# An S5 recurrence over chunks taken in two levels, with its local part on diagonal pair blocks

## The chip, the cores and the metric

The kernel runs on one core of a Trainium2 chip as a single launch. The metric is the device time of one execution in microseconds (us); the median of several executions is compared. TensorE (PE), VectorE (DVE), ScalarE (ACT) and GpSimd (POOL) each work through their own list of instructions in order, SyncE (SP) issues most of the loads, and the engines wait for each other by semaphores.

## The reference, cut to what matters

The kernel is a two-layer decoder trunk on 256 tokens and 2048 channels: an S5 state-space layer, shared keys and values, then a sparse-attention layer. Every sub-layer is modulated by products of `c` with large weights (adaLN). The change is in the S5 layer, whose mixer is:

```python
def s5_mixer(h, ...):
    u, z = jnp.split(h @ w_in, 2, axis=-1)
    ug = u.reshape(B_, L, SSM_GROUPS, SSM_GROUP)          # 128 groups of 16 channels
    bu = einsum('blgc,gnc->blgn', ug, bb)                  # 64 complex states a group
    x = scan(x[t] = a * x[t-1] + bu[t])                    # over 256 tokens
    y = Re(einsum('blgn,gcn->blgc', x, c)) + d_skip * ug
    y = gelu(y)
    y = y * sigmoid(y @ w_glu + b_glu)
    return (y * silu(z)) @ w_out
# adaLN: shift, scale, gate = split(silu(c) @ mod_w + mod_b)
```

## The kernel before, in words

A float32 product is made of three matmuls per block of 128x128 weights and 256 tokens: the weights are split into a high part (`hi`, ACT, line 202) and a low part (`lo`, DVE, line 203), and `project_half` (lines 227 to 229) runs `hi` on the high and low parts of the activations and `lo` on the high part. A half block is 8 such triples, 24 matmuls, and needs one 512 KB load into a ring of 8 buffers (`raw`), 2 `hi` and 2 `lo`.

The adaLN products are made in blocks of 128 columns. Blocks 0 to 31 are made while u is computed. Of the rest, `PE_MODS` go to TensorE in pairs (`pe_mod_pair`, line 157, "m" in the plan; four loads of 512 KB and then two small sums at line 162), and `DVE_MODS` to VectorE (`dve_mod`, line 144, "d" in the plan; two loads and two instructions of 128x1024 a block, which need the table `cact`).

The first half of u (8 blocks) is computed row by row (`u_rows`, lines 290 to 293). While that runs, the tables of the S5 layer are made. Then comes the S5 stage proper. The 256 tokens are cut into 64 chunks of 4 tokens, and the channels into two halves, f = 0 and 1:

- `u_turn` (line 516) brings u with the channels of pairs of groups on the partitions, and `scan_in` (line 573) makes what each chunk adds to the states; ACT copies it into `VV[f]` (names `Vva`, `Vvb`).
- `scan_run` (lines 608 to 611) is the recurrence over chunks: 62 steps of four DVE instructions of 128x64, each step reading what the step before wrote.
- `scan_local` (line 623) adds what a token gets from its own chunk. Its tables are Toeplitz matrices of 64x64; they are laid out by writing `ktd` to DRAM (8 writes, line 487) and reading it back shifted (16 reads, line 587), on POOL's queue.
- `scan_out` (line 641) adds what the states carry, and `y_turn` (line 663) turns y round to channels and through the GELU. `y_split` (lines 219 and 220) makes its high and low parts for the next product, the GLU.

What fills the time of the recurrences is a plan, `PLAN`: a string for each of the slots that the program passes with `fill()`: "u" and "z" are half blocks of the projections u and z, "m" a TensorE pair, "d" a VectorE block. The plan sets the order in which instructions are handed to a scheduler; the scheduler and the tile pools set the order on each engine. In the kernel before, the second half of u is computed before the first recurrence ends, and the 16 blocks of z are spread over both recurrences; z has a tile of its own in the place of the input x (tag `zz`).

After the S5 stage come the GLU product (line 708 reads its sums), w_out (line 722; it adds to `x`, which line 718 loads again), keys and values, queries, attention, and the output.

Of the kernel before, what the change touches and what calls it, by code (L numbers as in the profile page):

```python
# [70 lines left out]
def trunk_kernel(ctx, tc, xT, crow, ccol, vec, m0n, mn, mt, w_ur, w_in, w_glu, w_out, w_kv, w_qr, w_q, w_g,  # L71
# [113 lines left out]
    # ---------------------------------------------------------------- projections  # L185
# [8 lines left out]
    def split_w(r, n):  # L194
        """The first n of the eight blocks in r, four by four."""
# [11 lines left out]
    class Act:  # L207
        """A matrix [2048 channels, 256 tokens] as a high and a low part."""
# [37 lines left out]
    def rms_scale(tot):  # L246
        """1 / sqrt(mean square over channels), for every token, on all partitions."""
# [16 lines left out]
    # ---------------------------------------------------------------- layer 0: modulation and u  # L264
# [858 lines left out]
```

## Time and profile before

| | |
|---|---|
| median of 3 runs | 1364.55 us (1359.84, 1364.55, 1367.36) |
| span of the profiled execution | 1368.1 us, clock of TensorE 0.965 of full speed on average |
| time of the profiled execution itself | not on record apart from its span |
| busy: PE, DVE, ACT, POOL | 1267.0, 1068.3, 681.7, 42.5 us |
| chain that ended last, by engine | PE 68%, DVE 15%, DMA 12%, issue 3%, ACT 2% |
| HBM traffic | 326.10 MB read, 4.72 MB written |

PE is busy for 93% of the span, but the busy time of pipelined matmuls overlaps; the table by stage in the rows below shows where it is not busy. From the trace the stages are: u row by row and tables until 157 us, the S5 stage from there to about 428 us, the GLU to 527, w_out to 618, keys and values to about 845, then queries and attention. A duration in a row is that of one instruction; since matmuls are pipelined, the cost of many is read from the distance between their starts.

### The profile page before, as it was taken

What the parts mean: (1) busy time and instruction counts of PE and PEld (TensorE: products, weight loads), DVE (VectorE), ACT (ScalarE), POOL (GpSimd) and SP (SyncE); (2) the same over time, 40 slices, a digit from 0 to 9 for tenths busy, and PEclk for the clock granted to TensorE, in tenths of its full rate; (3) what the DMA queues carried; (4) which work ended last, traced back from release to release, by engine and by line L of the source; (5) the groups of instructions that cost most, each with busy time, mean ns of one, the idle gap of its engine ahead of it and who ended that gap; (6) DMA issues with size and microseconds to landing.
All of it is one profiled execution on the core that took longest, in us unless ns stands there. A gap on an engine that the chain in (4) does not pass through costs nothing.

```text
span 1368.1 us, 31424 instructions
## 1 busy us (share of the span) xinstructions
PE 1267.0 (93%) x12270; PEld 1200.6 (88%) x12270; DVE 1068.3 (78%) x2612; ACT 681.7 (50%) x1439; POOL 42.5 (3%) x71
## 2 busy tenths in 40 slices
PE   2799979989999999997998999999999999999995
PEld 2678779878888999986997999999999999999995
DVE  5998318999997898889877878776878777777665
ACT  3345544423356555544453545555555555555653
POOL 1000500001001000000000000000000000000001
PEclk9999989999999999997899999999999999999998
DMA  9799966649788999985887888876555444444541
GB/s 359 275 347 336 316 200 200 205 172 336 242 300 299 321 357 318 327 305 187 293 303 248 277 295 289 274 253 227 170 193 194 165 144 141 159 142 161 186 155 62
DMA packets 94055, 332.88 MB, mean 243 GB/s; under 512 B 12785, under 2 KB 13025, under 8 KB 92881
## 3 DMA queue, kind: packets, MB, share of 16 engines
q1 hardware_dynamic: 91792, 321.45, 68.3%
q0 software_dynamic: 2112, 9.42, 2.1%
q8 instruction: 96, 1.57, 0.5%
q14 instruction: 55, 0.44, 0.1%
HBM read 326.10 MB, written 4.72 MB: 242 GB/s over the span
## 4 chain that ended last, share of the span: by engine, by line
PE 68%; DVE 15%; DMA 12%; issue 3%; ACT 2%; SPq 0%; DVEq 0%; ACTq 0%
PE acc L229 18%; PE acc L227 18%; PE acc L228 18%; DMA raw<-in_mt_dram 6%; DVE lo L203 3%; DMA raw<-in_w_in_dram 3%; DVE raw L144 2%; PE macc L157 2%; PE s L957 1%; DVE stab L608 1%; DMA mraw<-in_m0n_dram 1%; PE op L1008 1%; DVE stab L610 1%; PE kp L467 1%; DVE stab L609 1%
## 5 line engine op out<-in xcount | busy, mean ns | idle before, releaser
L202 ACT ACTIVATE hi<-raw 128x512 fp32r<-128x512 f32 x640 | 400.9, 631 | 466.1 <-PE acc L228 395.9
L203 DVE TENSOR_TENSOR lo<-raw,hi 128x512 fp32r<-128x512 f32 x640 | 435.0, 690 | 146.8 <-ACT hi L202 143.6
L228 PE MATMUL acc<-hq,hi 128*128 128x256 f32 x960 | 274.9, 286 | 0.0
L229 PE MATMUL acc<-hq,lo 128*128 128x256 f32 x960 | 271.5, 284 | 2.5 <-DVE lo L203 2.3
L227 PE MATMUL acc<-hq,hi 128*128 128x256 f32 x960 | 273.2, 285 | 0.4 <-ACT hi L202 0.4
L144 DVE SCALAR_TENSOR_TENSOR raw<-raw,cact 128x1024 f32<-128x1024 f32 x156 | 190.1, 1220 | 57.0 <-DMA raw<-in_mt_dram 56.6
L229 PEld LDWEIGHTS acc<-hq,lo 128*128 128x128 f32 x960 | 180.5, 189 | 5.4 <-DVE lo L203 3.9
L228 PEld LDWEIGHTS acc<-hq,hi 128*128 128x128 f32 x960 | 180.9, 188 | 3.7 <-issue 3.3
L227 PEld LDWEIGHTS acc<-hq,hi 128*128 128x128 f32 x960 | 180.9, 188 | 1.3 <-issue 0.7
L229 PE MATMUL acc<-h,lo 128*128 128x256 f32 x384 | 114.0, 297 | 12.7 <-DVE lo L203 12.3
L229 PE MATMUL acc<-hkv,lo 128*128 128x256 f32 x384 | 114.2, 299 | 5.1 <-DVE lo L203 4.6
L227 PE MATMUL acc<-hkv,hi 128*128 128x256 f32 x384 | 112.5, 295 | 4.9 <-ACT hkv L260 4.9
L227 PE MATMUL acc<-h,hi 128*128 128x256 f32 x384 | 113.5, 296 | 1.0 <-ACT hi L202 1.0
L228 PE MATMUL acc<-hkv,hi 128*128 128x256 f32 x384 | 111.9, 294 | 0.8 <-DVE hkv L261 0.8
L228 PE MATMUL acc<-h,hi 128*128 128x256 f32 x384 | 111.6, 291 | 0.0
L229 PEld LDWEIGHTS acc<-h,lo 128*128 128x128 f32 x384 | 76.1, 198 | 17.4 <-DVE lo L203 14.0
L229 PEld LDWEIGHTS acc<-hkv,lo 128*128 128x128 f32 x384 | 77.3, 202 | 7.6 <-DVE lo L203 7.2
L227 PEld LDWEIGHTS acc<-hkv,hi 128*128 128x128 f32 x384 | 77.3, 202 | 5.8 <-ACT hkv L260 5.8
L227 PEld LDWEIGHTS acc<-h,hi 128*128 128x128 f32 x384 | 76.1, 198 | 5.3 <-issue 2.5
L228 PEld LDWEIGHTS acc<-hkv,hi 128*128 128x128 f32 x384 | 77.4, 202 | 1.4 <-DVE hkv L261 1.4
L157 PE MATMUL macc<-mraw,cz 128*32 128x128 f32 x1600 | 59.0, 300 | 18.9 <-DMA mraw<-in_m0n_dram 17.9
L228 PEld LDWEIGHTS acc<-h,hi 128*128 128x128 f32 x384 | 76.1, 198 | 0.1
(312 smaller groups left out, 2829.6 us busy)
## 6 DMA issues: line engine op xcount, KB each, us to landing
raw<-in_mt_dram SPq DMA_DIRECT2D x156, 512.0 KB, 5.6
raw<-in_w_z_dram SPq DMA_DIRECT2D x96, 512.0 KB, 3.7
mraw<-in_m0n_dram SPq DMA_DIRECT2D x64, 512.0 KB, 7.8
raw<-in_w_in_dram SPq DMA_DIRECT2D x48, 512.0 KB, 6.1
raw<-in_w_kv_dram SPq DMA_DIRECT2D x48, 512.0 KB, 5.2
mraw<-in_mn_dram SPq DMA_DIRECT2D x36, 512.0 KB, 6.6
raw<-in_w_glu_dram SPq DMA_DIRECT2D x32, 512.0 KB, 6.3
raw<-in_w_out_dram SPq DMA_DIRECT2D x32, 512.0 KB, 6.1
```

Of the source, the lines that this page charges most:

```text
L144: nc.vector.scalar_tensor_tensor(out=rf, in0=rf, scalar=1.0, in1=cact[:, 1024 * e:1024 * e + 1024], op0=OP.mult, op1=OP.mult, accum_out=mo ...
L157: nc.tensor.matmul(acc[32 * j:32 * j + 32, 128 * e:128 * e + 128], cz[:, q, :], r[:, q % 8, :], start=(e == 0 and q < 4), stop=(q >= 12), ...
L202: nc.scalar.activation(hi[:, 0:c, :], rr, AF.Copy)
L203: nc.vector.tensor_sub(lo[:, 0:c, :], rr, hi[:, 0:c, :].bitcast(F32))
L227: nc.tensor.matmul(acc, hi[:, kk, :], act(0, k), start=(k == 0), stop=False)
L228: nc.tensor.matmul(acc, hi[:, kk, :], act(1, k), start=False, stop=False)
L229: nc.tensor.matmul(acc, lo[:, kk, :], act(0, k), start=False, stop=(k == KT - 1))
L467: nc.tensor.matmul(kp[32 * q:32 * q + 32, l, :], bb[r][pr, 32 * h:32 * h + 32], kc_[pr, 2 * h:2 * h + 2, r, :], start=(l == 0 and r == 0), ...
L608: V.tensor_mul(ra, VH[:, :, :, :, k], ar)
L609: V.tensor_mul(rb, VH[:, :, ::-1, :, k], ai)
L610: V.tensor_add(ra, ra, VH[:, :, :, :, k + 1])
L957: nc.tensor.matmul(sp, qo(a, h)[:, qs], kk[:, kv, b, o:o + w], start=(i == 0), stop=(i == 2))
```

## The change

The chunks are kept, but the recurrence over 64 chunks goes in two levels. The chunk index is written as i (8 values, consecutive chunks) and s (8 segments), with s innermost. `scan_run` now does seven steps along i for all eight segments at once (four DVE instructions of 128x512 each), then six small steps that carry from segment to segment (128x64), and then adds to every chunk the carry times a power of the transition (16 instructions of 128x896). The powers are made by some 48 small DVE instructions (`powers`) earlier. So that s is innermost, the tokens are held in that order from the norm on (`order`, `into`), and the result goes back to token order where w_out's sums are added to `x`.

The Toeplitz tables, `scan_local` and the traffic through DRAM go. In their place `y_turn` adds the local part by products with 32x32 diagonal blocks (`kd`), four tiles beside each other, into the same PSUM tile that holds the turned y.

u is now held in the tile of the input (`x0`), and z is written over it; z can be computed only for blocks whose `y_turn` is done. All of z comes after the recurrences: 8 blocks in one slot after `y_turn(0)`, 8 after `y_turn(1)`. The rest of u and the pairs fill the recurrences. 14 more blocks of adaLN go to TensorE (`NA` 0 to 16, `NB` 2 to 0: `PE_MODS` from 18 to 32 blocks, `DVE_MODS` from 78 to 64), and `cact` is loaded only after `y_turn(1)`. `dvec` is loaded by four small DMAs in place of one. The `x` for w_out has the tag `cb`, which before held `cbS` and now holds `scr`, the recurrence's scratch.

```diff
-NA, NB = 0, 2
+NA, NB = 16, 0
 PLAN = [
-    "zzm", "", "um", "u", "d", "z", "z", "d", "m", "z", "zu", "zz", "dm", "m", "zm", "zmz", "z", "mz", "zzzz",
...
+    "uu", "uu", "muu", "uu", "muu", "uu", "muu", "uu", "m", "", "m", "",
+    "m", "", "m", "", "", "m", "", "m", "", "m", "", "zzzzmzzzzmzzzzmzzzz", "", "", "", "m", "", "m", "", "mm",
...
+    ucm = x0.rearrange("p m (i j s) -> p m i j s", i=8, j=4)
+    scr = pool.tile([128, 4096], F32, tag="cb", name="scr")
...
     def scan_run(f):
-        for k in range(1, 63):
-            V.tensor_mul(ra, VH[:, :, :, :, k], ar)
-            V.tensor_mul(rb, VH[:, :, ::-1, :, k], ai)
-            V.tensor_add(ra, ra, VH[:, :, :, :, k + 1])
-            V.tensor_add(VH[:, :, :, :, k + 1], ra, rb)
+        def step(dst, add, src, n, t, w, u):
+            sh = (128, 2, 32, w)
+            V.tensor_tensor(ra[:, :, :, 0:w], src, QW[0][:, n, gsl].unsqueeze(1).unsqueeze(3).to_broadcast(sh), op=OP.mult)
+            V.tensor_tensor(rb[:, :, :, 0:w], u, SG[t][:, :, gsl].unsqueeze(3).to_broadcast(sh), op=OP.mult)
+            V.tensor_add(ra[:, :, :, 0:w], ra[:, :, :, 0:w], add)
+            V.tensor_add(dst, ra[:, :, :, 0:w], rb[:, :, :, 0:w])
+        for i in range(2, 9):
+            x = X[:, :, :, i % 8, :]
+            step(x, x, X[:, :, :, i - 1, :], 0, 0, 8, X[:, ::-1, :, i - 1, :])
...
+        for j in range(1, 7):
+            step(cy[:, :, :, j + 1:j + 2], X[:, :, :, 0, j:j + 1], cy[:, :, :, j:j + 1], 7, 1, 1, cy[:, ::-1, :, j:j + 1])
+        nc.scalar.activation(X[:, :, :, 0, :], cy, AF.Copy)
+        for hh in range(2):
...
+            for r in range(2):
+                x = X[:, r, g, 1:8, :]
+                for e in range(2):
+                    V.tensor_tensor(mt_, cy[:, r ^ e, g, :].unsqueeze(2).to_broadcast(sh), pw[e], op=OP.mult)
+                    V.tensor_tensor(x, x, mt_, op=OP.subtract if e and not r else OP.add)
...
     def y_turn(f):
+        for mp in range(4 * f, 4 * f + 4):
+            p = psb([128, 2, 8, 4, 8], "yt")
+            for j in range(4):
+                for g in range(4):
+                    nc.tensor.matmul(p[32 * g:32 * g + 32, :, :, j, :], turn[:, 32 * j:32 * j + 32],
+                                     U[:, 2 * mp:2 * mp + 2, g, :].rearrange("p m (i s) -> p m i s", i=8),
+                                     start=(j == 0), stop=False, skip_group_check=True)
+            for ml in range(2):
+                for d in range(4):
+                    for g in range(4):
+                        pr = slice(32 * g, 32 * g + 32)
+                        nc.tensor.matmul(p[pr, ml, :, d:4, :], kd[pr, 2 * mp + ml, d, :], ucm[pr, 2 * mp + ml, :, 0:4 - d, :],
+                                         start=False, stop=(d == 3), skip_group_check=True)
+            nc.scalar.activation(ycm[:, 2 * mp:2 * mp + 2].rearrange("p m j k -> p (m j k)"), p.rearrange("p m i j s -> p (m i j s)"), AF.Gelu_apprx_tanh)
             fill()
+        ydone[0] += 1
...
-    tz0 = load_tz(0)
-    tz1 = load_tz(1)
     scan_in(0)
+    scan_run(0)
+    for q in range(4):
+        fill()
     while ustate[0] < 2 * (16 - NR):
         u_half()
     u_turn(1)
-    scan_run(0)
-    scan_local(0, tz0)
     scan_in(1)
     scan_run(1)
-    scan_local(1, tz1)
+    for q in range(4):
+        fill()
+    scan_out(0, load_ct(0))
     fill()
     y_turn(0)
     y_split(0)
     fill()
-    scan_out(1, [load_ct(1, 0), load_ct(1, 1)])
+    scan_out(1, load_ct(1))
     y_turn(1)
+    cact = pool.tile([128, D], F32, tag="cact", name="cact")
+    nc.gpsimd.dma_start(cact, crow.to_broadcast((128, D)))
```

Three places show how the instructions move. The first is DVE at the end of the first recurrence; `Vva` and `Vvb` are the states of the two halves, `lo` the low parts of weights. Before, it reads:

```order
L610 TENSOR_TENSOR stab<-stab,Vva 128x64
L203 TENSOR_TENSOR lo<-raw,hi 128x512
L611 TENSOR_TENSOR Vva<-stab 128x64
L608 TENSOR_TENSOR stab<-Vva,stab 128x64
L609 TENSOR_TENSOR stab<-Vva,stab 128x64
L610 TENSOR_TENSOR stab<-stab,Vva 128x64
```

Now (lines 622 to 625 are a step, 643 and 644 the carries) DVE has these rows at the same place and, in the second fence, at the end of the second recurrence:

```order
L204 TENSOR_TENSOR lo<-raw,hi 128x512
L624 TENSOR_TENSOR scr<-scr,Vva 128x512
L204 TENSOR_TENSOR lo<-raw,hi 128x512
L625 TENSOR_TENSOR Vva<-scr 128x64x8
L204 TENSOR_TENSOR lo<-raw,hi 128x512
L631 COPY scr<-Vva 128x64
L622 TENSOR_TENSOR scr<-scr 128x64
```

```order
L643 TENSOR_TENSOR scr<-scr 128x896
L644 TENSOR_TENSOR Vvb<-Vvb,scr 128x16x56
L643 TENSOR_TENSOR scr<-scr 128x896
L221 TENSOR_TENSOR yhl_3943<-U,yhl_3943 128x256 x2
L644 TENSOR_TENSOR Vvb<-Vvb,scr 128x16x56
L204 TENSOR_TENSOR lo<-raw,hi 128x512 x4
L221 TENSOR_TENSOR yhl_3943<-U,yhl_3943 128x256 x6
```

Low parts of weights stand between the steps of the first recurrence as before; in the second recurrence there are none from its first step to its last, where before z and adaLN stood between its steps.

The second place is ACT and PE around `y_turn(0)`. PE before, in `scan_local` of the first half, with z (lines 227 to 229) between:

```order
L623 MATMUL tp<-U,cbS 64x64 x16
L157 MATMUL macc<-mraw,cz 32x128 x32
L623 MATMUL tp<-U,cbS 64x64 x19
L162 MATMUL macc<-ones,msum 128x1 x2
L623 MATMUL tp<-U,cbS 64x64 x13
L227 MATMUL acc<-h_160,hi 128x256
```

PE now, at the first piece of `y_turn(0)` (line 672 turns y, 679 adds the pair blocks, 163 ends a pair of adaLN):

```order
L158 MATMUL macc<-mraw,cz 32x128 x32
L672 MATMUL yt<-U,stab 32x16x8 x16
L679 MATMUL yt<-x_93,ey 32x256 x2
L163 MATMUL macc<-ones,msum 128x1 x2
L679 MATMUL yt<-x_93,ey 32x256 x2
L679 MATMUL yt<-x_93,ey 32x8x24 x4
```

ACT now, there (line 634 copies the carries of the second recurrence, 661 the outputs of the first half, 161 a pair's sums, 203 the high parts of the first block of z):

```order
L634 ACTIVATE Vvb<-scr 128x64x8
L661 ACTIVATE U<-yp_3534 128x4x128
L661 ACTIVATE U<-yp_3535 128x4x128
L161 ACTIVATE msum<-macc 128x256
L166 ACTIVATE modv<-macc,vecs 128x1 x2
L681 ACT_TABLE_LOAD
L681 ACTIVATE U<-yt 128x512
L220 ACTIVATE yhl_3943<-U 128x256 x2
L161 ACTIVATE msum<-macc 128x256
L203 ACTIVATE hi<-raw 128x512 x4
```

Half of the copies that `y_turn(0)` reads, and all of z's high parts, now stand behind a copy that waits for the carries of the other half.

The third place is SP's list where `x` is loaded for w_out. Before, it stood among the weights of the GLU:

```order
L190 DMA raw<-in_w_in_dram 128x1024 x3
L190 DMA raw<-in_w_glu_dram 128x1024 x3
L718 DMA x<-in_xT_dram 128x4096
L190 DMA raw<-in_w_glu_dram 128x1024 x3
L142 DMA raw<-in_mt_dram 128x1024 x4
```

Now it stands between the weights of z's first and second block:

```order
L156 DMA mraw<-in_mn_dram 128x1024 x28
L191 DMA raw<-in_w_in_dram 128x1024 x2
L737 DMA x<-in_xT_dram 128x4096
L191 DMA raw<-in_w_in_dram 128x1024 x2
L156 DMA mraw<-in_mn_dram 128x1024 x4
```

It writes the place of `scr`, so it waits until the second recurrence has read that for the last time.

## Rows read from the trace of the kernel before

**Rows 1.** The page: the span, and the busiest engine with its share.

```profile
span 1368.1 us, 31424 instructions
PE 1267.0 (93%) x12270; PEld 1200.6 (88%) x12270; DVE 1068.3 (78%) x2612; ACT 681.7 (50%) x1439; POOL 42.5 (3%) x71
```

**Rows 2.** Busy time by stretch: PE, PEld, DVE, ACT, POOL, clock, DMA share, GB/s.

```profile
157.00:202.00 45.00, 35.71 (x547) 28.65 (x546) 6.16 (x15) 17.93 (x35) 5.64 (x9) 0.85 0.78 205
202.00:291.00 89.00, 82.20 (x988) 75.26 (x986) 81.82 (x299) 39.62 (x68) 0.57 (x1) 0.94 0.57 193
291.00:382.00 91.00, 84.91 (x1210) 76.83 (x1211) 85.69 (x298) 35.35 (x71) 6.70 (x5) 0.94 0.80 280
...
428.00:527.00 99.00, 97.55 (x804) 96.44 (x804) 86.42 (x159) 54.21 (x100) 0.00 (x0) 1.00 0.94 332
...
626.00:845.00 219.00, 207.29 (x1599) 201.20 (x1600) 178.30 (x360) 108.02 (x211) 0.00 (x0) 0.94 0.78 264
```

**Rows 3.** First instruction of a recurrence step: ns min/median/max, first and last start.

```profile
L608 DVE TENSOR_TENSOR stab<-Vva,stab x62: 254/266/275, 201.5 to 289.5; 128x64 f32<-128x64 f32 x62
L608 DVE TENSOR_TENSOR stab<-Vvb,stab x62: 250/267/296, 291.5 to 378.0; 128x64 f32<-128x64 f32 x62
```

**Rows 4.** Timeline of DVE, two successive steps of the recurrence: start, duration.

```profile
201.55 0.27 DVE L608 TENSOR_TENSOR stab<-Vva,stab 128x64 f32<-128x64 f32 x1 [0.88 <-ACT Vva L578]
...
202.52 0.27 DVE L608 TENSOR_TENSOR stab<-Vva,stab 128x64 f32<-128x64 f32 x1
```

**Rows 5.** Groups of DVE by shape: count, busy us, mean ns, idle before.

```profile
L203 DVE TENSOR_TENSOR lo<-raw,hi 128x512 fp32r<-128x512 f32 x640 | 435.0, 690 | 146.8 <-ACT hi L202 143.6
L144 DVE SCALAR_TENSOR_TENSOR raw<-raw,cact 128x1024 f32<-128x1024 f32 x156 | 190.1, 1220 | 57.0 <-DMA raw<-in_mt_dram 56.6
...
L769 DVE TENSOR_TENSOR zk<-zk,vecs 128x240 f32<-128x240 f32 x16 | 8.5, 568 | 0.0
```

**Rows 6.** Chain of waits from 100 to 200 us: start, duration, what.

```profile
112.33 0.54 PE macc L162 x4
...
151.14 18.05 DMA raw<-in_w_in_dram
...
171.28 12.21 DMA raw<-in_w_in_dram
```

**Rows 7.** DMA issues: count, KB each, median us to landing.

```profile
x<-in_xT_dram SPq DMA_DIRECT2D x1, 2048.0 KB, 12.6
...
cact<-in_crow_dram POOLq DMA_DIRECT2D x1, 1024.0 KB, 14.0
ktd<-ey POOLq DMA_DIRECT2D x8, 64.0 KB, 5.5
cbS<-ktd POOLq DMA_DIRECT2D x4, 128.0 KB, 12.4
```

**Rows 8.** Busy time of a stretch of 25 us in attention, projections only.

```profile
1275.00:1300.00 25.00, 25.00 (x211) 25.00 (x210) 15.60 (x26) 15.39 (x27) 0.00 (x0) 1.00 0.56 190
```

**Rows 9.** Timeline of TensorE, one pair of adaLN.

```profile
124.07 1.95 PE L157 MATMUL macc<-mraw,cz 128*32 128x128 f32 x64
```

**Rows 10.** Timeline of TensorE's weight loads, turning y in four column tiles.

```profile
358.12 0.13 PEld L663 LDWEIGHTS yt<-U,stab 128*32 128x32 f32 x4 [0.30 <-issue]
358.55 0.13 PEld L663 LDWEIGHTS yt<-U,stab 128*32 128x32 f32 x4 [0.30 <-issue]
```

**Rows 11.** Timeline of TensorE in the first half's local part.

```profile
258.31 2.90 PE L623 MATMUL tp<-U,cbS 64*64 64x64 f32 x92
```

**Rows 12.** First and last start of the matmuls of u by rows.

```profile
L293 PE MATMUL uacc<-h,lo x128: 274/282/583, 43.5 to 157.4; 128*128 128x256 f32 x128
```

**Rows 13.** First and last start of ACT's reads of the GLU's sums.

```profile
L708 ACT ACTIVATE sg<-acc,vecs x16: 454/455/475, 434.0 to 521.7; 128x256 f32<-128x256 f32 x16
```

**Rows 14.** Stretches of 4 us around an idle TensorE, columns as in Rows 2.

```profile
188.00:192.00 4.00, 4.00 (x79) 3.88 (x76) 0.14 (x2) 3.01 (x7) 0.00 (x0) 0.50 0.60 237
...
196.00:200.00 4.00, 4.00 (x123) 3.72 (x125) 0.69 (x1) 1.35 (x4) 0.00 (x0) 1.00 0.54 151
```

More of the change, by code (lines that the diff above doesn't have):

```diff
@@ L253, in rms_scale, with norm_mod @@
         return rstd
-    def norm_mod(xt, rstd, scol, bcol, act, ks=range(KT)):
+    def norm_mod(xt, rstd, scol, bcol, act, ks=range(KT), order=lambda a: a, into=lambda a: a):
         for k in ks:
             xn = tk("xn")
-            nc.vector.scalar_tensor_tensor(xn, in0=xt[:, k, :], scalar=scol[:, k:k + 1], in1=rstd, op0=OP.mult, op1=OP.mult)
+            nc.vector.scalar_tensor_tensor(into(xn), in0=order(xt[:, k, :]), scalar=scol[:, k:k + 1], in1=order(rstd),
+                                           op0=OP.mult, op1=OP.mult)
             nc.scalar.activation(act(0, k), xn, AF.Identity, bias=bcol[:, k:k + 1])
@@ L273, in trunk_kernel, with order, into @@
     scol = pool.tile([128, KT], F32, tag="scol", name="scol", bufs=2)
+    def order(a):
+        return a.rearrange("p (s q) -> p q s", q=32)
+    def into(a):
+        return a.rearrange("p (q s) -> p q s", q=32)
     def mod_pair(k):
@@ L300, in trunk_kernel @@
             mod_pair(k + SK)
-        norm_mod(x0, rstd0, scol, modv[:, 0:16], h0, (k,))
+        norm_mod(x0, rstd0, scol, modv[:, 0:16], h0, (k,), order, into)
         u_rows(k)
@@ L411, in trunk_kernel @@
     V.tensor_scalar(bc[:, 1, :, 1, :], bc[:, 1, :, 1, :], -1.0, None, op0=OP.mult)
-    dmat = stab[:, 1952:1968]
-    nc.gpsimd.dma_start(dmat, dvec)
-    ktd = tc_dram(tc, ctx, "ktd", [16, 2, 64, 64])
+    dmat = stab[:, 1952:1968].rearrange("p (x y) -> p x y", y=2)
+    for g2 in range(2):
+        for y in range(2):
+            nc.gpsimd.dma_start(dmat[64 * g2:64 * g2 + 64, :, y].rearrange("p (s l) -> p s l", l=2),
+                                dvec.rearrange("p (s g l) -> p s g l", g=2, l=2)[64 * y:64 * y + 64, :, g2, :])
     ctd = tc_dram(tc, ctx, "ctd", [128, 32, 2, 64])
@@ new lines, in trunk_kernel @@
+    scr = pool.tile([128, 4096], F32, tag="cb", name="scr")
+    ra, rb, cy = [scr[:, 512 * i:512 * i + 512].rearrange("p (r g s) -> p r g s", r=2, s=8) for i in range(3)]
+    mt_ = scr[:, 1536:2432].rearrange("p (g i s) -> p g i s", g=16, i=7)
+    QW = [scr[:, 2432 + 512 * i:2944 + 512 * i].rearrange("p (i g) -> p i g", i=8) for i in range(2)]
+    SG = [scr[:, 3456 + 128 * i:3584 + 128 * i].rearrange("p (r g) -> p r g", r=2) for i in range(2)]
+    w1, w2_ = [scr[:, 3712 + 192 * i:3904 + 192 * i] for i in range(2)]
@@ new lines, in powers @@
+    def powers():
+        for t, a in zip(QW, (PR, PI)):
+            V.tensor_copy(t[:, 0, :], a[:, :, 3])
+        for n in (1, 2, 4):
+            d = [[t[:, n + x, :] for t in QW] for x in range(n)]
+            for x in range(0, n):
+                ar, ai = [t[:, x, :] for t in QW]
+                br, bi = [t[:, n - 1, :] for t in QW]
+                u1, u2 = w1[:, 0:64], w2_[:, 0:64]
+                V.tensor_mul(u1, ar, br)
+                V.tensor_mul(u2, ai, bi)
+                V.tensor_sub(d[x][0], u1, u2)
+                V.tensor_mul(u1, ar, bi)
+                V.tensor_mul(u2, ai, br)
+                V.tensor_add(d[x][1], u1, u2)
+        for t, i in zip(SG, (0, 7)):
+            V.tensor_scalar(t[:, 0, :], QW[1][:, i, :], -1.0, None, op0=OP.mult)
+            V.tensor_copy(t[:, 1, :], QW[1][:, i, :])
@@ L496, in trunk_kernel @@
+    powers()
     pick = stab[:, 832:1104]
@@ L558, in fill @@
         slot[0] += 1
-    cbS = pool.tile([128, 2, 2048], F32, tag="cb", name="cbS")
     def scan_in(f):
@@ L592, in load_ct @@
-    def load_ct(f, q):
+    def load_ct(f):
         if f == 0:
-            return ctA[:, q]
-        ct = cbS[:, q].rearrange("p (g r m) -> p g r m", g=16, r=2)
-        nc.gpsimd.dma_start(ct, ctd[:, 16 * q:16 * q + 16])
-        return ct
-    ra = stab[:, 192:256].rearrange("p (h r b) -> p h r b", r=2, b=2)
-    rb = stab[:, 256:320].rearrange("p (h r b) -> p h r b", r=2, b=2)
+            return ctA
+        ct = pool.tile([128, 2, 16, 2, 64], F32, tag="ca", name="ct1")
+        for q in range(2):
+            nc.gpsimd.dma_start(ct[:, q], ctd[:, 16 * q:16 * q + 16])
+        return ct
```

148 lines of the change are left out of this document (50 added, 98 removed), and 10 rows, old and new, of the table PLAN.

## The prediction

> **What bounds the kernel now.** I read the page first: TensorE is busy for 93% of a span of 1368.1 us [rows 1], so a gain must come from the stretches in which it is not. The table by stretch shows where these are [rows 2]. In the GLU PE is busy 97.55 of 99 us, so nothing is to be had there. In the S5 stage it stands idle for 9.3 us of 157 to 202, 6.8 of 202 to 291 and 6.1 of 291 to 382. In the last two DVE is busy 81.82 of 89 and 85.69 of 91 us: the two recurrences last from 201.5 to 289.5 and from 291.5 to 378.0 [rows 3], and all work of u, z and adaLN fills them. So DVE sets the length of these 180 us and PE is only filled up to it. The start of the stage has a different limit: the chain of waits goes through two loads of weights of 18.05 and 12.21 us [rows 6], far above the usual time of a load, beside the writes of `ktd` (8 of 5.5 us) and shifted reads of it (12.4 us for 128 KB) and a `cact` of 14.0 us [rows 7].
>
> **Prices.** One step of the old recurrence starts 0.97 us after the one before [rows 4], so one DVE instruction of 128x64 in a chain costs 0.97 / 4 = 0.2425 us. 128x512 costs 0.69, 128x1024 1.22 us [rows 5]; 128x896 is put between them at 0.69 + 0.53 x 384/512 = 1.08. In a stretch of projections alone 211 matmuls fill 25 us [rows 8], 0.1185 us each, 5.69 for a block of 48. A pair of adaLN takes 1.95 us [rows 9] and its two sums about 0.5 [rows 6], 2.45 together. Four column tiles of 32 run beside each other: four instructions of 512 columns start every 0.43 us [rows 10] (a program matmul in float32 is two instructions). Two diagonal tiles of 64x64 with 64 columns give one instruction per 0.0315 us (2.90 / 92) [rows 11].
>
> **The change part by part.** The profiled execution has its span alone, 1368.1 us, 3.5 above the median; I work out differences in its clock and take them from the median 1364.55.
>
> *The recurrence itself.* Removed: 62 x 0.97 = 60 us of DVE chain a half. Added: 28 x 0.69 = 19.3, carries 24 x 0.2425 = 5.8, and 16 x 1.08 = 17.3, in all 42.4 us. So DVE gives back about 18 us a half, not the factor that the count of steps (62 to 13) suggests. The some 48 small instructions of the powers (11.6 us) lie in the tail of u by rows, where DVE is busy 6.16 of 45 us just behind [rows 2].
>
> *The start of the stage.* The last row of u ends at 157.4 [rows 12]. Until the first step of the first recurrence PE has 6 half blocks of u (144 x 0.1185 = 17.1), `u_turn` (64 instructions / 4 x 0.43 = 6.9), `scan_in` (256 x 0.0315 = 8.1) and a pair (2.45), with 1.5 for the last copy: 157.4 + 36.1 = 193.5, before 201.5. The DRAM traffic of `ktd` and the `cact` load are gone from here; if loads are as late as before, the end of this range is 201.5, and if the six half blocks don't delay the `scan_in` it is 177.
>
> *First recurrence and the rest of u.* PE has 240 matmuls and 2 pairs, 33.3 us, to 227; beside it DVE has 28 x 0.69 and 16 low parts of 0.69, 30 us. Then DVE's carries and corrections, 23.1 us, to about 248 (the copies of the states add 1 or 2), while PE does `u_turn(1)`, `scan_in(1)` and two pairs (17.5). So the second recurrence starts at about 248, before 291.5. Its steps and carries end at 273, its corrections at 290.
>
> *What is late next.* Between 248 and 273 PE has only the 128 products of the first half's `scan_out` (8.1) and some pairs: z can't be computed, since its tile is u's until `y_turn(0)` is done. And `y_turn(0)` itself must wait: ACT's list has the copy of the second half's carries ahead of half the copies that `y_turn(0)` reads. Queued behind it on ACT are the sums of a pair, the GELU and the high parts of the first z. So `y_turn(0)` starts at 273 and takes 4 x 3.5 = 14 us (by [rows 10]: 32 instructions of 128 columns and 64 that add up to 2,560 columns a tile give 3.0 each, plus 0.5 for the hand-over) and two pairs 4.9. After some 10 us of idling PE's clock is at 0.50, as at 188 to 192, and back at 1.00 by 196 [rows 14]: 3.5 more. The first z is done at about 296. The second waits for a load that stands on SP behind the 2 MB `x`, which waits for the corrections' end at 290; `x` took 12.6 us [rows 7], so z goes on from 303 (between 296, if z's loads overtake its transfer, and 310, if they share it badly). Seven z blocks and three pairs, 47 us: 351. `scan_out(1)` and `y_turn(1)`, 26: 377. Eight z and two pairs, 50.4: 427. Before, the first sum of the GLU was read at 434.0 [rows 13], a block of 5.69 earlier is 428.3. So the stage ends at the same place: what the recurrence gives back is lost because z no longer covers it.
>
> *Later stages.* 21 of the 28 instructions of 128x1024 that DVE no longer does were in the S5 stage; counted by program order seven fewer stand behind it, each 1.30 with its read of the accumulator and 0.5 MB of loads. Most were in the keys and values, where PE is idle 11.7 of 219 us [rows 2]. The bounds are 0 (hidden behind PE) and 7 x 1.30 = 9.1, or 12 with the loads; I take 8, since PE waits there for low parts.
>
> *New token order and small edits.* The copies of u and z become contiguous, `norm_mod` writes strided, `x` is read by columns of 32 in w_out: 48 instructions off the path, from -2 to +4, taken as 0. The four small loads of `dvec` lie on POOL's queue beside u by rows, with a hundred us of cover; `cact` moves to the second block of z, where DVE has no adaLN yet; 14.0 us [rows 7] beside 50 us of z.
>
> Sum: -1 for the stage, -8 or 9 for what follows, about -10: 1354.
>
> **The rivals.**
>
> R1, the waits are hidden. All PE work of the stage is 24 blocks of 5.69, 16 pairs of 2.45, two turns of 6.9, four times 8.1 and two `y_turn` of 14, some 250 us; from 157.4 that is 407, if the scheduler lets pairs and z fill. That is 20 us earlier: 1334. For it: half of the waits are guessed from a list, and DVE ends 46 us earlier than z is needed. Against it: z truly needs `y_turn(0)`.
>
> R2, slower: elements in short runs. The new steps read and write runs of 8 in larger strides, with an operand repeated along them. The dearest DVE row of such a kind is 128x240 in 568 ns, 2.37 ns an element [rows 5], against 1.35 for 512 in 0.69. By that a 512 costs 1.21 and the 8 corrections that write states 2.12: 28 x 0.52 + 8 x 1.04 = 23 us more in a half. It decides as soon as the first recurrence ends after `scan_in(1)`: the carries that `y_turn(0)` waits for come 23 + 14.6 = 37 later, about 1390. Against it: it is one row, its runs and repeats are its own, and of the old steps, whose 64 elements all lie apart, 266 ns [rows 3] is mostly fixed cost and tells little.
>
> R3, the pair blocks serialise. Their four tiles have different rows and columns but write one PSUM tile. If they go one by one, a piece costs 0.86 + 4 x 2.15 = 9.5 in place of 3.0, a half 38 in place of 14, twice 24.5: 1403. Against it: the two diagonal tiles of the old local part also wrote one tile of PSUM, and took 0.0315 an instruction [rows 11]; one tile alone would need 0.43 x 64/512 = 0.054 by the rate of [rows 10], so the two overlapped.
> The Trainium skill, *TensorEngine Tiling (Array Packing)*, "Gotcha 1: PSUM Pressure", says "Different row tiles cannot access same PSUM bank simultaneously"; by it R3 would hold. The trace does not agree for two tiles of 64, and no row shows four of 32.
>
> R4, nothing comes out. The block on SP costs its upper end (310) and the saved adaLN is hidden: the stage ends at 427 + 7 = 434, 6 later than before, and what comes back later is of the same size: about 1364. That the change does less than it says is part of this: only 14 blocks move (18 to 32), and what they save on DVE they cost on PE, 7 x 2.45 = 17 us, in a kernel that PE bounds.
>
> **How the numbers follow.** Half a per cent (6.8 us) is about what a measurement of this kernel can tell from no change. The forecast, 1354, has .48, with its own range from 1343 to 1365 (start of the stage from -10 to +6, later stages from -12 to 0); R1 .25; R4 .12; R2 .10; R3 .05. Faster by over 0.5% (below 1357.7): all of R1 and 0.30 of the forecast, .55. Slower (above 1371.4): R2, R3 and a tail of .03, .18. The same: .27. The range from 1328 to 1384 takes in R1 and R4 and leaves out most of R2 and R3.
>
> **What would show it.** In the profile after: the first instruction of the first recurrence at about 194 and of the second at about 248; 0.69 for 128x512 in the steps and 1.08 for the corrections (R2: 1.2 and 2.1); idle PE before `y_turn(0)` ended by ACT; `x` issued when the second recurrence ends, and a wait of z for loads of w_in behind it; pair blocks at 3 to 3.5 us a piece (R3: 9.5); first GLU sum at about 433 (R1: below 415). The forecast is wrong if PE is not idle between 248 and 300, or if the stage ends elsewhere than 420 to 436.

## The result: slower by 1.2%

The changed kernel takes 1378.6 us (median of 4 runs, 1375.6 to 1384.57) against 1363.49 us of the kernel before: a ratio of 1.0115, with a 95% interval of 1.0084 to 1.0146. The forecast was 1354 us, faster, so its sign was wrong. That 1378.6 lies within the stated range of 1328 to 1384 us is luck: the range was that wide for the rivals, and the forecast's own ended at 1365. Of the two profiles, the one after is 14.8 us longer. The page of the changed kernel (answers to [rows 1]):

```profile
span 1382.9 us, 32898 instructions
```

The stages with the same columns as [rows 2], moved by the time that each begins later, and last the stretch of the second recurrence up to `y_turn(0)`:

```profile
161.00:202.00 41.00, 41.00 (x583) 34.62 (x581) 15.53 (x32) 19.84 (x47) 0.00 (x0) 1.00 0.49 168
202.00:291.00 89.00, 80.75 (x1449) 70.28 (x1452) 81.50 (x143) 28.84 (x71) 1.06 (x2) 0.87 0.70 246
291.00:390.00 99.00, 96.70 (x1706) 88.34 (x1698) 39.18 (x74) 41.20 (x89) 3.56 (x14) 0.97 0.69 249
...
642.00:862.00 220.00, 205.21 (x1603) 198.84 (x1604) 180.15 (x362) 109.55 (x217) 0.00 (x0) 0.94 0.78 261
254.00:282.00 28.00, 21.35 (x468) 19.19 (x462) 26.84 (x56) 4.87 (x15) 1.06 (x2) 0.74 0.80 295
```

VectorE, which was the busy engine from 291 to 382 us (85.69 of 91), is now busy 39.18 of 99 us there: it no longer sets the length. TensorE has no gap at all up to 202 us and is busy 96.70 of the 99 us from 291 on. Between these, beside the second recurrence, it waits as the prediction said: it is busy 21.35 of 28 us, at a mean granted clock of 0.74. The marks of the recurrence, the last row of u and the first sum of the GLU (first and last start in the changed kernel; answers to [rows 3, 12, 13]):

```profile
L622 DVE TENSOR_TENSOR scr<-Vva,scr x7: 680/682/691, 197.4 to 220.7; 128x512 f32<-128x512 f32 x7
L622 DVE TENSOR_TENSOR scr<-Vvb,scr x7: 691/693/694, 254.1 to 270.1; 128x512 f32<-128x512 f32 x7
...
L643 DVE TENSOR_TENSOR scr<-scr x16: 1091/1092/1093, 231.7 to 294.6; 128x896 f32<-128x896 f32 x16
...
L302 PE MATMUL uacc<-h,lo x128: 274/281/581, 46.0 to 161.0; 128*128 128x256 f32 x128
...
L727 ACT ACTIVATE sg<-acc,vecs x16: 454/457/477, 446.1 to 537.3; 128x256 f32<-128x256 f32 x16
```

The second recurrence starts at 254.1 us where it started at 291.5. Yet the first sum of the GLU is read at 446.1, before at 434.0. From the last row of u to that sum it is 285.1 us, before 276.6: in these two profiles the S5 stage lost 8.5 us. The start of the kernel lost 3.6 (161.0 against 157.4), and all that follows 2.7 (936.8 against 934.1).

The table has the same marks for all kernels that were run. Its columns run from mark to mark: the last start of a matmul of u by rows; from there to ACT's first read of a GLU sum; to VectorE's first read of a sum of w_out; to its last such read; to its last write of a key; to the end of the span. A single profile is good to some 4 us in the column of u (the ten with `dvec` in four pieces end u between 157.6 and 164.0), and to less in the S5 stage: the kernel before took 276.6 us there and, with nothing but an empty tile more, 283.6 (e13). So the 8.5 us alone are not clear of what profiles differ by. The step between nine pairs in the changed kernel (258.6 to 264.3) and sixteen (278.9 to 287.3) is well clear of it.

| profile | pairs on TensorE | last row of u | S5 stage | GLU | w_out | to last key | rest |
|---|---|---|---|---|---|---|---|
| before | 9 | 157.4 | 276.6 | 93.3 | 90.0 | 193.3 | 557.5 |
| after | 16 | 161.0 | 285.1 | 96.3 | 92.0 | 194.8 | 553.7 |
| e1 x by POOL | 16 | 160.6 | 279.9 | 98.3 | 92.8 | 196.0 | 552.0 |
| e2 y_turn(0) early | 16 | 161.2 | 285.1 | 99.0 | 93.7 | 198.9 | 552.3 |
| e3 before + adaLN | 16 | 155.5 | 293.6 | 106.7 | 85.6 | 191.5 | 552.8 |
| e4 9 pairs, even slots | 9 | 164.0 | 263.3 | 91.1 | 85.4 | 204.0 | 550.7 |
| e5 even slots | 16 | 157.7 | 280.9 | 93.4 | 87.6 | 192.9 | 550.2 |
| e6 after, no recurrence | 16 | 159.4 | 284.1 | 98.2 | 96.0 | 199.9 | 554.6 |
| e7 before, no recurrence | 9 | 156.9 | 268.1 | 91.4 | 87.8 | 186.6 | 555.5 |
| e8 dvec in one | 16 | 156.9 | 286.5 | 96.2 | 94.6 | 188.5 | 551.7 |
| e9 9 pairs, old slots | 9 | 158.8 | 262.6 | 94.3 | 98.8 | 213.9 | 550.6 |
| e10 before, even slots | 9 | 153.8 | 283.9 | 92.6 | 92.7 | 201.4 | 551.9 |
| e12 two pairs late | 16 | 161.5 | 287.3 | 91.1 | 88.2 | 196.6 | 550.7 |
| e11 e4 + dvec in one | 9 | 158.4 | 264.3 | 88.8 | 84.9 | 198.9 | 542.0 |
| e13 before + 64 bytes | 9 | 154.9 | 283.6 | 89.7 | 88.1 | 189.6 | 548.4 |
| e14 after + 64 bytes | 16 | 157.6 | 278.9 | 96.5 | 96.5 | 191.7 | 543.7 |
| e15 e4 + 64 bytes | 9 | 161.8 | 258.6 | 90.7 | 84.9 | 202.0 | 541.5 |
| e16 e11 + x by POOL | 9 | 156.7 | 261.3 | 90.7 | 84.9 | 199.9 | 541.3 |

### The profile page after: what moved, and what is told of

Same layout as the page of the kernel before. It is cut to its first block, busy times and chain, and to the rows that moved or that the text cites. A ratio compares the mean times of both kernels' runs of the same rounds, so it can differ in the third digit from the quotient of the medians.

```text
span 1382.9 us, 32898 instructions
## 1 busy us (share of the span) xinstructions
PE 1286.8 (93%) x13194; PEld 1222.9 (88%) x13194; DVE 1021.4 (74%) x2228; ACT 678.4 (49%) x1473; POOL 18.2 (1%) x44
## 4 chain that ended last, share of the span: by engine, by line
PE 74%; DVE 11%; DMA 11%; issue 2%; ACT 2%; SPq 0%; DVEq 0%; ACTq 0%
PE acc L230 19%; PE acc L228 18%; PE acc L229 18%; DMA raw<-in_mt_dram 8%; DVE lo L204 3%; PE macc L158 3%; DMA raw<-in_w_in_dram 2%; PE yt L679 1%; DVE raw L145 1%; PE s L976 1%; DMA mraw<-in_m0n_dram 1%; PE vp L597 1%; PE ut L544 1%; PE op L1027 1%; PE kp L473 1%
## 5 line engine op out<-in xcount | busy, mean ns | idle before, releaser
L204 DVE TENSOR_TENSOR lo<-raw,hi 128x512 fp32r<-128x512 f32 x640 | 431.8, 688 | 188.5 <-ACT hi L203 172.4
L145 DVE SCALAR_TENSOR_TENSOR raw<-raw,cact 128x1024 f32<-128x1024 f32 x128 | 156.3, 1221 | 64.5 <-DMA raw<-in_mt_dram 64.3
L230 PE MATMUL acc<-h,lo 128*128 128x256 f32 x384 | 109.1, 284 | 0.2 <-DVE lo L204 0.2
L228 PE MATMUL acc<-h,hi 128*128 128x256 f32 x384 | 109.2, 284 | 0.0
L229 PE MATMUL acc<-h,hi 128*128 128x256 f32 x384 | 108.2, 282 | 0.0
L158 PE MATMUL macc<-mraw,cz 128*32 128x128 f32 x2048 | 73.1, 299 | 24.8 <-DMA mraw<-in_m0n_dram 20.1
L158 PEld LDWEIGHTS macc<-mraw,cz 128*32 128x32 f32 x2048 | 60.6, 120 | 31.7 <-issue 20.0
L230 PE MATMUL acc<-yhl,lo 128*128 128x256 f32 x256 | 73.2, 288 | 3.4 <-DVE lo L204 3.2
L230 PE MATMUL acc<-ghl,lo 128*128 128x256 f32 x256 | 72.2, 283 | 3.3 <-DVE lo L204 3.3
```

What stands on the lines that cost most here:

```text
L145: nc.vector.scalar_tensor_tensor(out=rf, in0=rf, scalar=1.0, in1=cact[:, 1024 * e:1024 * e + 1024], op0=OP.mult, op1=OP.mult, accum_out=mo ...
L158: nc.tensor.matmul(acc[32 * j:32 * j + 32, 128 * e:128 * e + 128], cz[:, q, :], r[:, q % 8, :], start=(e == 0 and q < 4), stop=(q >= 12), ...
L204: nc.vector.tensor_sub(lo[:, 0:c, :], rr, hi[:, 0:c, :].bitcast(F32))
L228: nc.tensor.matmul(acc, hi[:, kk, :], act(0, k), start=(k == 0), stop=False)
L229: nc.tensor.matmul(acc, hi[:, kk, :], act(1, k), start=False, stop=False)
L230: nc.tensor.matmul(acc, lo[:, kk, :], act(0, k), start=False, stop=(k == KT - 1))
```

## Experiments: the work moved, or the waits?

Theory B: the seven pairs that moved to TensorE cost what they take, and nothing comes back. Theory A: the stage is long because z starts late, behind `y_turn(0)`.

**e1**, the load of `x` off SP's queue:

```diff
-    nc.sync.dma_start(x, xT)
+    nc.gpsimd.dma_start(x, xT)
```

> The changed kernel with one edit: the x for w_out is loaded on POOL's queue in place of SP's, so that z's weights no longer stand behind it. Theory A (the stage is long because z starts late, and the load on SP is one of the reasons): z's second block, which got its high part at 307.8 us, gets it at about 300, and the kernel gains 5 to 8 us, about 1371. Rival B (the work moved to TensorE sets the length, and TensorE reached that block only at 308.3 anyway): 0 to 2 us, about 1377.

Measured: 1380.38 us, ratio 1.0121 (1.0080 to 1.0163). The stage was 5 us shorter in that profile, the total was not. This is what B forecast.

**e2**, nothing of `y_turn(0)` behind the second recurrence:

```diff
-        nc.scalar.activation(X[:, :, :, 0, :], cy, AF.Copy)
+        nc.gpsimd.tensor_copy(X[:, :, :, 0, :], cy)
...
     scan_in(1)
-    scan_run(1)
-    for q in range(4):
-        fill()
     scan_out(0, load_ct(0))
     fill()
     y_turn(0)
+    for q in range(4):
+        fill()
+    scan_run(1)
...
-    nc.sync.dma_start(x, xT)
+    nc.gpsimd.dma_start(x, xT)
```

> The changed kernel with three edits: scan_out(0) and y_turn(0) stand ahead of the second recurrence in program order, the copy of the carries is made by POOL in place of ACT, and x is loaded on POOL's queue. So nothing that y_turn(0) needs waits for the second recurrence. Theory A: y_turn(0), which began at 281.8 us, begins at about 262 to 265, but z's low parts still stand behind the second recurrence on VectorE, which ends at 297; z starts at about 298 in place of 302.6 and its second block without a wait; gain 5 to 10 us, about 1371. Rival B: the pairs that stand there fill TensorE up to the same time, gain below 3 us.

Measured: 1392.13 us, 1.0197 (1.0167 to 1.0227), a stage of 285.1 as before the edit. The first pair block came at 273.2 us (275.3 in the changed kernel), so the copy was not what that one waited for. What the copy held was the next instruction: in the changed kernel TensorE stood 4.9 us for a pair's sums, which ACT makes behind the copy. That wait is gone in e2, and the first matmul of z came at 296.5 us in place of 302.6. Yet the last block of z was done no earlier (copied at 438.6 us, in the changed kernel at 438.3). Why the later stages took more time is open. A's gain isn't there.

**e3**, the adaLN part alone, on the kernel before:

```diff
-NA, NB = 0, 2
+NA, NB = 16, 0
...
-    mod_finish(96, 32)
+    mod_finish(96 + NA, 32 - NA)
```

> The kernel before with only the adaLN part of the change (NA, NB = 16, 0: 32 blocks on TensorE in place of 18, 64 on VectorE in place of 78), S5 stage and plan as before. Theory B (moved blocks cost TensorE what they take and nothing comes back): 14 blocks are 7 pairs of 2.45 us, 17 us, slower by 8 to 17 us, 1372 to 1380. Theory A (they are free, the S5 rewrite is what costs): within 5 us of before, 1360 to 1368; the forecast's own price for the later stages, -8, would make it 1356.

Measured: 1391.61 us, 1.0190 (1.0158 to 1.0222): 26 us for 14 blocks, more than B's 8 to 17. The stage took 293.6 us, 17.0 more, with 13 of the 16 pairs in it, and the GLU 13.4 more with the other three (this view groups TensorE from 443 to 550 us: busy, mean):

```profile
L157 PE MATMUL macc<-mraw,cz 128*32 128x128 f32 x192 | 6.7, 275 | 0.0
```

Only w_out and what follows gave 4 and 6 us back.

**e4**, the changed kernel without the adaLN part; to have 32 blocks done ahead of the keys and values, VectorE gets one in every slot of GLU and w_out:

```diff
-NA, NB = 16, 0
+NA, NB = 0, 2
...
-    "d", "", "dd", "d", "d", "", "d", "d", ...
-    "d", "", "", "d", "d", "d", "", "d", "", "", "d", "", "d", "", "d", "",
+    "d", "d", "dd", "d", "d", "d", "d", "d", ...
+    "d", "d", "d", "d", "d", "d", "d", "d", "d", "d", "d", "d", "d", "d", "d", "",
```

> The changed kernel without the adaLN part of the change (NA, NB = 0, 2: 18 blocks on TensorE, 78 on VectorE), with the blocks that must be done before the keys and values put into the empty slots of GLU and w_out. Theory B: the S5 stage gets 14 to 17 us shorter since seven pairs leave the two stretches of z, where TensorE has no gap; GLU and w_out become bound by VectorE (8 to 9 blocks more of 2.6 us, of which their gaps take about half), 5 to 15 us longer; in sum 1365 to 1378. Theory A: the S5 stage stays within 5 us, since its length is set by waits, and later stages get longer, in sum 1385 or more.

Measured: 1349.84 us, 0.9896 (0.9862 to 0.9930). The stage fell by 22 us to 263.3. But GLU and w_out did not grow, they fell to 91.1 and 85.4: two edits were in it, so they were taken apart.

**e5**, the two plan lines alone, 16 pairs kept. 

> The changed kernel, all 16 pairs kept, with the one other edit of the run before it: a VectorE block of adaLN in every slot of GLU and w_out (the same 64 blocks, done earlier). It tells whether that run was faster for its seven missing pairs or for its fuller slots. Theory B (pairs): GLU and w_out stay at 96 and 98 us or shrink by no more than 5 together, S5 stage at 279 us, total 1373 to 1380. Rival C (slots: VectorE waits 15 us for loads of the uneven blocks, low parts behind it): GLU and w_out 91 us each, 12 us shorter, total 1364 to 1370.

Measured: 1368.39 us, 1.0026 (1.0004 to 1.0048): 12 us faster than the changed kernel, with a stage of 280.9. From here to e4 it is 1.0026 / 0.9896, 1.3%, 18 us for seven pairs. In the changed kernel VectorE stands in the GLU before loads of uneven blocks, with low parts behind them (idle us, times, longest; 440 to 536 us of the changed kernel, then 421 to 512 of e4; in e5 it is 6.5 us, from 432.5 to 528.5):

```profile
DVE raw L145 <- DMA raw<-in_mt_dram: 15.0, 13, 3.1
```

```profile
DVE raw L145 <- DMA raw<-in_mt_dram: 4.3, 4, 1.5
```

**e9**, the fewer pairs alone, with the old slots (the first diff of e4 only). 

> The changed kernel with 18 blocks of adaLN on TensorE (seven pairs fewer), but with the plan of GLU and w_out as the changed kernel has it; the VectorE blocks that this leaves over are done in one piece ahead of the keys and values. With the run of the evened plan alone it separates pairs from slots. Theory B+C (seven pairs cost about 17 us, the uneven slots about 12, and they add): S5 stage about 258 us as in the run with both, GLU and w_out about 96 and 98, and some 7 blocks of 2.6 us in a piece before the keys and values that TensorE waits for: total 1370 to 1380. If the evened slots alone made that run fast, the same total as the changed kernel, 1379 or more, with an S5 stage near 279.

Measured: 1382.0 us, 1.0118 (1.0087 to 1.0148). The stage is 262.6 as in e4, so these 20 us belong to the pairs and not to the slots. All of it is lost again where the blocks that are left over are done in a piece: w_out 98.8, and 213.9 to the last key.

**e10**, even slots in the kernel before:

```diff
-    ... "d","m","m","d","dmd","","d","","dm","d","","d","dm","","d","", ...
+    ... "d","md","md","d","dmd","d","d","d","dm","d","d","d","dm","d","d", ...
```

> The kernel before with one edit: a VectorE block of adaLN in every slot of GLU and w_out (its two stages took 93 and 96 us). Theory C: uneven slots cost the kernel before too, both stages go to 91 to 92 us, total 1354 to 1360; then the S5 rewrite alone is worth what is left between this and the run of the changed kernel with fewer pairs and even slots (0.990 of before), 5 to 10 us. Rival: the kernel before gains nothing from it (1362 or more), and the S5 rewrite without its adaLN part is worth the whole 14 us.

Measured: 1380.16 us, 1.0111 (1.0076 to 1.0147). Even slots are no gain by themselves; why this kernel loses by them (w_out 92.7, 201.4 to the last key) wasn't found. Its stage of 283.9 is like that of e13, 283.6. So it isn't settled how much of e5's 12 us belongs to the changed kernel.

**e6 and e7**, both recurrences left out, in either kernel:

```diff
-    scan_run(0)
...
-    scan_run(1)
```

> The changed kernel with both recurrences left out (the states stay as each chunk alone makes them). Theory B: the second recurrence is all that y_turn(0) and z wait for, y_turn(0) begins at about 258 in place of 282 us and z at 275 in place of 303; what TensorE has to do is then 250 us of 161 on, so the GLU starts at 415 to 420 in place of 440; total 1354 to 1360. Theory A in its strong form (waits are most of the loss): 30 us or more, below 1350.

> The kernel before with both recurrences left out in the same way. TensorE's work in its stage is some 235 us from 157.4, so if the recurrence is what stretches it to 271 us, the stage ends up to 30 us earlier: 1335 to 1345 (theory: DVE set the length of the stage before). Rival: TensorE and the loads fill it anyway, 1355 or more. The difference to the same run of the changed kernel tells what the change costs apart from any recurrence: by theory B 15 to 20 us.

Measured: e6 1391.41 us, 1.0181 (1.0146 to 1.0215); e7 1344.33 us, 0.9839 (0.9804 to 0.9874). In the kernel before the recurrence cost 22 us, of which its stage shows 8.5 (268.1 us). In the changed kernel it costs nothing: without it the stage is 284.1 us, and the whole took 0.7% more than with it, in the stages behind, which is not explained. Both of my theories had foreseen a gain in e6. The chain of e6 shows what holds z without any recurrence (start, duration, what):

```profile
276.47 6.79 DMA raw<-in_w_in_dram
283.35 1.15 ACT hi L203 x2
284.49 0.28 ACT msum L161
284.82 1.01 PE macc L163 x4
285.83 3.92 PE yt L679 x47
```

and SP's queue there (start, duration, issues):

```profile
229.02 42.38 SPq L156 DMA_DIRECT2D mraw<-in_mn_dram  x20
276.47 2.12 SPq L191 DMA_DIRECT2D raw<-in_w_in_dram  x4
```

Twenty loads for five pairs go first; z's first weights are issued at 276.47; ACT waits for them ahead of a pair's sums, and TensorE waits for these in the middle of `y_turn(0)`. In this chain what holds z is the pairs.

**e12**, two pairs moved from between the pieces of `y_turn(0)` to among the last eight blocks of z, on e5:

```diff
-    "m", "", "m", "", "", "m", "", "m", "", "m", "", "zzzzm...", "", "", "", "m", "", "m", "", "mm",
+    "m", "", "m", "", "", "m", "", "", "", "", "", "zzzzm...", "", "", "", "m", "", "m", "", "mmmm",
```

> The changed kernel with even slots and all 16 pairs, two of them moved from between the pieces of y_turn(0) to behind the last z. Theory D (beside its 2.45 us a pair costs waits there: its four loads hold half of the ring, so z's first weights are issued late, and ACT waits for them ahead of the pair's own sums): y_turn(0) and the first z without the waits of 4 to 8 us, total 1360 to 1364 against 1368.4 of the even run. Rival B (only TensorE's time counts, wherever a pair stands): 1366 to 1372.

Measured: 1373.95 us, 1.0063 (1.0038 to 1.0088). The first z came at 302.4 in place of 306.4 us, as theory D had it, but the last at 441.0 in place of 431.6. D fell as a way to save time: a pair costs its time at either place. The total is even above what B forecast, and that is open.

## Experiments: the start, and where tiles lie

**e8**, one load of `dvec`:

```diff
-    for g2 in range(2):
-        for y in range(2):
-            nc.gpsimd.dma_start(dmat[64 * g2:..., :, y]..., dvec...[64 * y:..., :, g2, :])
+    nc.gpsimd.dma_start(stab[:, 1952:1968], dvec)
```

> The changed kernel with dvec loaded in one piece as before (the skip terms then belong to other channels). In the changed kernel the first adaLN weights landed at 20.6 us against 18.9 before, while the DMA moved 261 against 385 GB/s between 15 and 20 us. If the four loads of single words cause that, the first landing goes back to about 18.9 and the last row of u from 161.0 to 157.5 to 159; if not, both stay.

Measured (one run, 1376.08 us): the first adaLN product at 17.6 us (18.6 in the changed kernel, 17.6 in the one before), u from 43.5 to 156.9, and 405 GB/s from 15 to 20 us. In the changed kernel the transfers crawl beside the single words (15 to 20 us, columns as in [rows 2]; the kernel before moved 385 GB/s there):

```profile
15.00:20.00 5.00, 1.08 (x16) 0.66 (x16) 3.70 (x17) 0.92 (x4) 0.00 (x0) 1.00 1.02 261
```

**e11**, e4 with that load in one piece, laid out by four matmuls:

```diff
+    dv = pool.tile([128, 16], F32, name="dv")
+    nc.gpsimd.dma_start(dv, dvec)
+    dp = psc([128, 2, 8], "dp")
+    for y in range(2):
+        for g2 in range(2):
+            o = 64 * y
+            nc.tensor.matmul(dp[64 * g2:64 * g2 + 64, y], ident[:, o:o + 64], dv...[:, :, g2, :], ...)
+    nc.scalar.activation(dmat.rearrange("p x y -> p y x"), dp, AF.Copy)
```

> The changed kernel with 18 blocks of adaLN on TensorE, even slots in GLU and w_out, and dvec loaded in one piece and brought to its layout by four small matmuls, so that no single words are loaded. Theory: as the run without that last edit (1349.8 us, 0.990 of before), less the 3 to 4 us that the start gains when the first weights land at 18.9 in place of 20.6 us: 1344 to 1349, last row of u at 157 to 158 in place of 161 to 164.

Measured: 1336.15 us, 0.9780 (0.9750 to 0.9810). 14 us in place of 3 to 4, and mostly in stages that the edit does not touch: 1275 to 1300 us holds 223 matmuls ([rows 8]: 211).

**e13, e14, e15**, the same 64 bytes a partition as an empty tile (and a memset of it), in the kernel before, the changed one and e4:

```diff
+    pad = pool.tile([128, 16], F32, name="pad")
+    V.memset(pad, 0.0)
```

> The kernel before with one empty tile of 64 bytes a partition (and a memset of it) at the place where the last but one run had its staging tile for dvec. In that run projections from some activations took 0.112 us a matmul in place of 0.1185 (223 in 25 us in place of 211), though nothing in them was changed. Theory E (where the later tiles lie decides): the same here, GLU 89 us in place of 93, 223 matmuls in 25 us near the end, total 1350 to 1356. Rival (it was the chip, or the smoother start): 211 matmuls, 1361 to 1369.

> The changed kernel with the same empty tile of 64 bytes. Theory E: 8 to 12 us less than the changed kernel's 1.0115 of before, 1.002 to 1.006; if tiles did not lie well in the changed kernel and do in the one before, the two padded kernels come out nearer to each other than 10 us. Rival: 1.009 to 1.014.

> The changed kernel with 18 blocks of adaLN on TensorE and even slots (0.990 of before), with the same empty tile and dvec still loaded in four pieces. The run with dvec in one piece and a staging tile came to 0.978. Theory E: 0.978 to 0.983 here as well, so that the single words of dvec cost 0 to 5 us. Rival: 0.988 to 0.992, and the whole 14 us are the start's.

Measured: 0.9948 (0.9916 to 0.9981), 1.0021 (0.9993 to 1.0049) and 0.9814 (0.9766 to 0.9861): 7, 13 and 11 us less than each had without the tile. In e13, where nothing else was changed:

```profile
1275.00:1300.00 25.00, 25.00 (x223) 25.00 (x223) 16.50 (x28) 16.64 (x30) 0.00 (x0) 1.00 0.56 197
```

So where the later tiles lie sets the pace of some matmuls, in all three kernels alike; between the padded two the change still costs 0.7% (1.0021 / 0.9948). It isn't what made the change slow. But these two profiles lose the time elsewhere: the stage of e14 is 4.7 us shorter than that of e13, and its GLU and w_out, with the uneven blocks, take 193.0 us against 177.8. From e15 to e11 3 to 5 us are left for the single words, within the intervals.

**e16**, e11 with `x` by POOL. 

> The kernel of 0.978 (18 blocks on TensorE, even slots, dvec in one piece) with x loaded on POOL's queue in place of SP's. With seven pairs fewer, TensorE waits from 254 to 300 us for the second recurrence and for z's weights. If the load on SP holds z up there, 3 to 6 us less: 0.974 to 0.976; if z's first weights wait for the ring alone, 0.977 to 0.980.

Measured: 1336.11 us, 0.9791 (0.9736 to 0.9846), no difference to e11. e11 and e16 beat both kernels.

## Why the prediction was wrong

Two terms of the sum failed. The stage with its start was put at -1: the first sum of the GLU was read at 446.1 us, before at 434.0, so it came to +12.1. The later stages were put at -8 for the seven instructions that VectorE is spared, and came to +2.7. The step behind both is that VectorE sets the pace: "DVE sets the length of these 180 us and PE is only filled up to it", and "PE waits there for low parts". So the path through the stage was added up from waits behind VectorE, and work taken off VectorE was counted as a gain. The runs showed TensorE's own work in its place. Without either recurrence, some 120 us of VectorE's chain, the stage of the kernel before is 268.1 us in place of 276.6 (e7). TensorE's busy time in the stage, up to the first block of the GLU, in the kernel before, the changed one and e4 (columns as in [rows 2]):

```profile
157.40:428.30 270.90, 246.95 (x3259) 217.85 (x3258) 213.07 (x695) 118.54 (x222) 17.13 (x28) 0.94 0.73 241
```

```profile
161.00:440.40 279.40, 267.08 (x4187) 241.33 (x4186) 164.15 (x293) 116.44 (x254) 4.62 (x16) 0.95 0.68 240
```

```profile
164.00:421.50 257.50, 246.22 (x3704) 223.41 (x3703) 165.44 (x294) 112.73 (x233) 4.79 (x16) 0.95 0.58 206
```

TensorE is idle for 24.0, 12.3 and 11.3 us of these. So the rewrite took some 12 us of idle time out, and the seven pairs put some 20 us of work in. All work of TensorE there, 250 us in R1, kept it busy for 267.08, part of it at a granted clock of 0.50, the lower of its two levels, behind waits like that of 4.9 us before 280.8 us.

- **The prices were right.** 128x512 took 0.68 to 0.69 us, 128x896 1.09 (forecast 0.69 and 1.08); from 254.1 to the end of the corrections at 297.4 it is 43.3 us (42.4). Rival R2 fell. A piece of `y_turn` took 1.01 + 2.31 us (forecast 3.0 to 3.5), in the chain of the changed kernel, where the first piece runs at a granted clock of 0.50:

```profile
281.83 4.40 PE yt L679 x46
286.23 2.71 PE macc L158 x64
...
293.19 1.01 PE yt L672 x32
294.20 2.31 PE yt L679 x64
```

  R3 fell: four 32x32 tiles on different rows wrote one tile of PSUM beside each other, 64 instructions in 2.31 us, where R3 had 8.6. The Trainium skill, *TensorEngine Tiling (Array Packing)*, "Gotcha 1: PSUM Pressure", says that different row tiles cannot access the same PSUM bank simultaneously; these tiles show no such cost, and the measurement decides.
- **"What is late next" named the wrong cause.** The marks of its path were 193.5 us for the first recurrence, 248 for the second, 273 for the end of the carries, 303 for z's second block, 351 and 377 before and behind `scan_out(1)` and `y_turn(1)`, and 427 for the end of the stage. They came at 197.4, 254.1, 278.9, 308.5, 356.8, 385.1 and 440.4: 3.6 us late from the start, and some 8 more behind 356.8. The waits were there (`y_turn(0)` behind the copy of the carries, `x` issued at 297.5). But e1 and e2 took the causes away and gained nothing in all, and e6 took the recurrence away and the stage stayed at 284 us. Work on TensorE and the loads of its pairs fill the time up to z anyway. (The first z "done at about 296" is where the forecast's own terms end `y_turn(0)`; a block of 5.69 more is 301. The path goes by 303, so nothing hangs on it.)
- **The rewrite and the moved blocks had to be priced apart.** With nine pairs in both, the stage went from 276.6 us (283.6 in e13) to 263 (e4, e9): the rewrite is worth 13 us there, or more. With sixteen it is 279 to 287: 20 us, 2.6 to 2.9 a pair by total and by stage, forecast 2.45 in the path. The forecast had the two cancel at -1; they came to +8.5 in the two profiles above, and to -4.7 between the padded two, so their difference isn't known to better than that. That the blocks leave VectorE cost, not helped: the rewrite puts `cact` where it can't be used until `y_turn(1)` is done, so 14 blocks lose the cover of the recurrence and must go somewhere: to TensorE (18 us, e5 to e4), in a piece (nothing left, e9), or into even slots (e4, a gain).
- **"Later stages, 8"** was +2.7, a miss of 10.7 beside the 13 of the stage's end. It took TensorE's gaps in the keys and values for waits on VectorE's adaLN. With seven instructions fewer the gaps there are 14.8 of 220 us, before 11.7 of 219, and in the GLU VectorE now waits 15 us for loads of those that are left. Where the net loss stands differs between pairs of profiles: between the padded two it is in the GLU and w_out. With the same instructions behind the stage, e2 takes 7 and e6 12 us more there than the changed kernel, and why is open.
- **"`dvec` ... with a hundred us of cover"**: its own wait is covered, its traffic is not. First rows of u at 45.7 to 46.5 us with four loads of single words, at 43.2 to 44.2 without, in every profile: some 2 us.
- The last sentence of R4, that the blocks cost 17 us on TensorE in a kernel that TensorE bounds, came nearest, at a chance of .12 and in a rival priced at 1364; the forecast had put these 17 us into the sum and then let VectorE pay them back. The chance of .18 for a slower kernel came from R2 and R3, which both fell, and a tail of .03: no part of the prediction leads to the measured time.

## What to carry to other kernels

In this kernel, where one engine is busy for 93% of the span, work that moved to it was paid in full, and work taken from the others paid only where that engine waited for exactly that: look for the row that shows it. A recurrence that is made short frees nothing if the work that lay beside it loses its place: ask where each filler goes, and price the two apart. Before a wait is called the limit, look at what stands behind it: here its removal showed the same stage from another cause twice (e2, e6), and in e1 the same total. And before a stage is blamed for a few us, look at how much it moves when nothing in it was changed: here 7 us.

## What the hardware showed that was not expected

- One more tile of 64 bytes a partition brought projections from 211 to 223 matmuls in 25 us (0.1185 to 0.1121 us each), and 7 to 13 us in three kernels. Only some activations gain: in e13 the mean of a matmul on `qo` fell from 283 to 276 ns, on `yhl` (the GLU) from 284 to 278, on `ghl` (w_out) by 1 to 3. Why was not tried.
- Four loads of single words of 2 KB each brought the transfers beside them from 385 to 261 GB/s for 5 us, at a full DMA share (1.02) in both; with one load in place of the four (e8) it was 405.
- The recurrence of 128x512 steps in runs of eight words cost no more than plain instructions of that size: 0.68 to 0.69 us against 0.69 for the low parts.
